# Hard-max attention on one core: row runs per partition, transposes in 32 small units, and a plain end loop

## The chip, the cores and the metric

The kernel runs on one core of one Trainium2 chip. The core has a matrix engine (TensorE, PE in the profile, with its weight loads as PEld), a vector engine (VectorE, DVE), an activation engine (ScalarE, ACT), a general engine that also issues indirect DMAs (GpSimd, POOL) and a sync engine that issues DMAs (SP). Each engine runs its own instructions in order and waits for the others on semaphores. The metric is the device time of one execution in microseconds (us).

## The reference

```python
def setup_inputs():
    B, Sq, Sk, D = 4, 4096, 4096, 128
    return {"q": randn(B, Sq, D), "k": randn(B, Sk, D), "v": randn(B, Sk, D)}   # float32

def reference(q, k, v):
    logits = np.matmul(q, k.transpose(0, 2, 1))
    best = np.argmax(logits, axis=-1)
    b_idx = np.arange(q.shape[0])[:, None]
    return v[b_idx, best, :].astype(np.float32)
```

For each of 4 x 4096 queries the key with the largest dot product is found, and the value row of that key is the output. There is no softmax.

## The kernel before, in words

A tile is 128 queries, one to a partition; there are T = 128 tiles, 32 (NQT) to a batch. Keys are taken in groups of four neighbours. For each tile the kernel finds the best group with reduced precision, then the best key of the group, and then fetches that key's value row. Rows where this could be wrong (close rows) are computed again in fp32.

**Screening on PE, ACT and VectorE.** kT and qT hold the transposed keys and queries of a batch in fp16, in two buffers each, so that the next batch is prepared while this one runs. kT holds four blocks of 1024 columns, a column being a group: block 0 and 1 are sum and difference of the group's first two keys, block 2 and 3 those of the other two. `screen(t)` (lines 216 to 220) issues for one half x of the blocks `dpart` (difference product, whose absolute value A is taken by ACT, L198) and `spart` of the tile before (sum product, L189, plus A through an identity matmul, L208). Half 0 goes through ACT as E (L211), half 1 stays in PSUM; `fold` (L224, VectorE) takes the larger of both into the upper 16 bits of W, whose lower 16 bits hold the group's number and were written once by an iota (L111). `top` (L227, VectorE) takes the eight largest of W. All PSUM tiles come in turn from one pool of four buffers of 1024 fp32 columns (tag "u", line 44), the small ones of the transposes too.

**Refining on VectorE and POOL.** `gather` reads the best group of each query from a table of key differences k16 by an indirect DMA per tile (L244, POOL, "kg"). `dots` multiplies with the queries and sums (L259 to L268), for two tiles at a time. `pick` (L278 to L298) works on a chunk of 8 tiles (4 near the end): it finds the best of the four keys, counts how many are near it (near, CNT), and computes the row of v (win). One indirect DMA per tile (L301, POOL, "vr") fetches the value rows; SP stores a chunk of them (L305). The k16 table is written by `put_k`: a VectorE product kd (L72) and an SP store (L75).

**Close rows.** After half of the tiles `flag_segment`, and after the rest `flags_first` and `flags_last`, collect the rows that are too close (two small matmul groups L349/L350 and L372, in the end phase L450, L465, L491), read their record (FR), query (FQ) and three groups of keys (FK) by indirect DMAs, compute exactly (`exact`, L516 to L535), fetch the value rows (FV) and scatter them over the output. The scatter has to come after all stores of the ordinary rows. `all_rows` is a fallback that the input of this case doesn't enter.

**What sets the order.** The program text does, engine by engine. The loop over `it` (lines 657 to 682) issues for tile `it`: loads on POOL (keys of the next batch at qt 2 to 9, queries at qt 12 to 19), one transposing unit (`unit_k`, 512 columns, at qt 10 to 17; `unit_q`, 512 columns, at qt 18 to 25), the screening, the fold of the tile before, one step of each of the waiting generators (dots, pick, flags; `step`), the top of the tile before that, its gathers, and in `issue` one "kg" and one "vr" gather on POOL. In batch 0 `trn_q` brings 1024 columns of queries at tiles 2, 4 and 6. Before the loop `trn_half` transposes the first keys (lines 148 to 154).

A transposing matmul of keys writes every fourth column of its PSUM tile, since a partition of natk holds 16 neighbouring keys, that is four groups:

```python
o = ps[:, m::4]                                                 # unit_k
nc.gpsimd.iota(out=W.bitcast(U16)[:, 0::2], pattern=[[-1, NG]], base=NG - 1, channel_multiplier=0)
```

Tile t of a batch holds the queries t * 128 to t * 128 + 127, one to a partition, so a query load or an output store has runs of one row (512 bytes in fp32).

After the loop (lines 684 to 726) the end phase is written out by hand: the last tops, all group gathers that are left ahead of the value gathers, then for each chunk its dots, its pick and some value gathers; for the last chunk the counts first, then the close rows' work, whose record and query gathers go ahead of the last three (LATE) value gathers; two of these follow the key gathers, one follows FV, and the scatter is last.

Of the kernel before, what the change touches and what calls it, by code (L numbers as in the profile page):

```python
# [20 lines left out]
QSCALE = 128.0  # L21
TAU = 8.0
NEAR = 0.5
LATE = 3
# [3 lines left out]
def kernel(ctx, tc, q, k, v, out):  # L28
# [36 lines left out]
    def load_q(b, x, y):  # L65
        nc.gpsimd.dma_start(out=natq[b % 2][:, x:y], in_=q[b].rearrange("(t p) d -> p t d", p=P)[:, x:y])  # L66
# [43 lines left out]
    for W in W_t:  # L110
        nc.gpsimd.iota(out=W.bitcast(U16)[:, 0::2], pattern=[[-1, NG]], base=NG - 1, channel_multiplier=0)  # L111
# [31 lines left out]
    def trn_half(b, u, h):  # L143
        x = 2 * (u // 2)
        if h == 0:
            tk_t[u] = pp.tile([P, 1024], FP32, tag="u", name=f"tk_{b}_{u}")
        ps = tk_t[u]
        for m in range(4):
            o = ps[:, h * 512 + m:(h + 1) * 512:4]
            nc.tensor.matmul(out=o, lhsT=natk[b % 2][:, h, 4 * m + x, :], rhs=identh, start=True, stop=False)  # L150
            nc.tensor.matmul(out=o, lhsT=natk[b % 2][:, h, 4 * m + x + 1, :],
                             rhs=identn if u % 2 else identh, start=False, stop=True)
        if h == 1:
            nc.scalar.activation(out=kT[b % 2][:, u * 1024:(u + 1) * 1024], in_=ps, func=AF.Copy)

    def unit_k(b, u, h):
        x = 2 * (u // 2)
        ps = pp.tile([P, 512], FP32, tag="u", name=f"uk_{b}_{u}_{h}")
        for m in range(4):
            o = ps[:, m::4]  # L160
# [3 lines left out]
        nc.scalar.activation(out=kT[b % 2][:, u * 1024 + h * 512:u * 1024 + (h + 1) * 512], in_=ps, func=AF.Copy)  # L164

    def unit_q(b, g):
        ps = pp.tile([P, 512], FP32, tag="u", name=f"uq_{b}_{g}")
        for i in range(4):
            nc.tensor.matmul(out=ps[:, i * P:(i + 1) * P], lhsT=natq[b % 2][:, g * 4 + i, :], rhs=identh,  # L169
                             start=True, stop=True)  # L170
        nc.scalar.activation(out=qT[b % 2][:, g * 512:(g + 1) * 512], in_=ps, func=AF.Copy, scale=QSCALE)  # L171
# [61 lines left out]
    def gather(c, t0, n):  # L233
# [16 lines left out]
        start(dots(c, t0, n), "dots", c)  # L250
# [20 lines left out]
    def pick(c, t0, t1):  # L271
# [8 lines left out]
        near = sp.tile([P, n, 4], FP32, tag=f"near{n}", name=f"near_{c}")  # L280
        nc.vector.scalar_tensor_tensor(out=near, in0=d, scalar=NEAR, in1=mx.to_broadcast([P, n, 4]),
                                       op0=OP.add, op1=OP.is_ge)
        yield "dve",
        nc.vector.tensor_reduce(out=CNT[:, t0:t1], in_=near, axis=AX_X, op=OP.add)
        done.add(("cnt", c))
        yield "cnt",
# [17 lines left out]
        def store():  # L304
            nc.sync.dma_start(out=out[b, qt * P:(qt + n) * P, :].rearrange("(j p) d -> p j d", p=P), in_=vr)  # L305
            done.add(("out", c))

        stores.add(store)
        late_q.append(store)

# [5 lines left out]
    def flag_segment(t0, t1, ready, stored):  # L316
# [62 lines left out]
        nc.vector.scalar_tensor_tensor(out=rw[:, 1:2], in0=tp[:, 0:1], scalar=float(P), in1=tp[:, 1:2], op0=OP.mult, op1=OP.add)  # L379
        yield "dve", 0.17  # L380
        row = fp.tile([P, 1], U32, tag="row", name=f"row_{t0}")
        nc.vector.scalar_tensor_tensor(out=row, in0=rw[:, 1:2], scalar=-float(P), in1=rw[:, 0:1], op0=OP.add, op1=OP.add)
# [44 lines left out]
    LF = {}  # L427

    def flags_first(t0, t1):
        S = t1 - t0  # L430
        H = LF["H"] = fp.tile([P, S, 4], U32, tag="H", name="H_e")
        nc.vector.tensor_scalar(out=H, in0=TOP.bitcast(U32)[:, t0:t1, 0:4], scalar1=16, scalar2=None,
                                op0=OP.logical_shift_right)
        F = LF["F"] = fp.tile([P, S], FP32, tag="F", name="F_e")
        nc.vector.scalar_tensor_tensor(out=F, in0=H[:, :, 1], scalar=TAU, in1=H[:, :, 0], op0=OP.add, op1=OP.is_ge)

    def flags_last(t0, t1, win_last, late):
        S = t1 - t0
        H, F = LF["H"], LF["F"]
        nc.vector.scalar_tensor_tensor(out=F, in0=CNT[:, t0:t1], scalar=1.5, in1=F, op0=OP.is_gt, op1=OP.max)  # L440
        Ec = fp.tile([P, S], FP32, tag="Ec", name="Ec_e")
        nc.vector.tensor_tensor(out=Ec, in0=F, in1=codes[:, t0:t1], op=OP.mult)
        e8 = fp.tile([P, 8], FP32, tag="e8", name="e8_e")
        nc.vector.max(out=e8, in_=Ec)
        val = fp.tile([P, 8], FP32, tag="val", name="val_e")
        nc.vector.tensor_scalar(out=val, in0=e8, scalar1=0.5, scalar2=None, op0=OP.is_gt)
        n2 = fp.tile([P, 3], FP32, tag="n2", name="n2_e")
        nc.vector.tensor_reduce(out=n2[:, 0:1], in_=val, axis=AX_X, op=OP.add)  # L448
        ps = pp.tile([P, 1024], FP32, tag="u", name="fp_e")
        nc.tensor.matmul(out=ps[:, 0:1], lhsT=tri, rhs=n2[:, 0:1], start=True, stop=True)  # L450
        win_last()
        bs = fp.tile([P, 1], FP32, tag="bs", name="bs_e")
        nc.vector.tensor_copy(out=bs, in_=ps[:, 0:1])
        posn = fp.tile([P, 8], FP16, tag="posn", name="posn_e")
        nc.vector.scalar_tensor_tensor(out=posn, in0=iota_r[:, 0:8], scalar=bs, in1=val, op0=OP.add, op1=OP.mult)
        rec2 = fp.tile([P, 8, 2], BF16, tag="rec2", name="rec2_e")
        nc.vector.tensor_copy(out=rec2[:, :, 0], in_=e8)
        nc.vector.tensor_copy(out=rec2[:, :, 1], in_=iota_p.to_broadcast([P, 8]))
        OH = fp.tile([P, 8, P], BF16, tag="OH", name="OH_e")
        for z in range(2):  # L460
            nc.vector.tensor_tensor(out=OH[:, 4 * z:4 * z + 4], in0=iota_h.unsqueeze(1).to_broadcast([P, 4, P]),
                                    in1=posn[:, 4 * z:4 * z + 4].unsqueeze(2).to_broadcast([P, 4, P]), op=OP.is_equal)
        ps2 = pp.tile([P, 1024], FP32, tag="u", name="fq_e")
        for s in range(8):
            nc.tensor.matmul(out=ps2[:, 0:2], lhsT=OH[:, s, :], rhs=rec2[:, s, :], start=s == 0, stop=s == 7)  # L465
        nc.vector.tensor_reduce(out=n2[:, 1:2], in_=F, axis=AX_X, op=OP.add)
        tp = fp.tile([P, 2], FP32, tag="tp", name="tp_e")
        nc.vector.tensor_copy(out=tp, in_=ps2[:, 0:2])
        rw = fp.tile([P, 2], FP32, tag="rw", name="rw_e")
        nc.vector.tensor_scalar(out=rw[:, 0:1], in0=tp[:, 0:1], scalar1=0.5, scalar2=float(1 << 20), op0=OP.is_lt, op1=OP.mult)  # L470
        rr = fp.tile([P, 1], U32, tag="rr", name="rr_e")
        nc.vector.scalar_tensor_tensor(out=rr, in0=tp[:, 1:2], scalar=float(T), in1=tp[:, 0:1], op0=OP.mult, op1=OP.add)
        nc.vector.scalar_tensor_tensor(out=rr, in0=rr, scalar=-1.0, in1=rw[:, 0:1], op0=OP.add, op1=OP.add)
        nc.vector.scalar_tensor_tensor(out=rw[:, 1:2], in0=tp[:, 0:1], scalar=float(P), in1=tp[:, 1:2], op0=OP.mult, op1=OP.add)
        row = fp.tile([P, 1], U32, tag="row", name="row_e")
        nc.vector.scalar_tensor_tensor(out=row, in0=rw[:, 1:2], scalar=-float(P), in1=rw[:, 0:1], op0=OP.add, op1=OP.add)

        def get(dst, src, idx, hi):
            nc.gpsimd.indirect_dma_start(out=dst, out_offset=None, in_=src, in_offset=IOA(ap=idx, axis=0),
                                         bounds_check=hi - 1, oob_is_err=False)  # L480

        late(max(0, len([g for g in late_q if g not in stores]) - LATE))
        get(FR, rec, rr, P * T)
        get(FQ, q_flat, row, P * T)
        bo = fp.tile([P, 1], U32, tag="bo", name="bo_e")
        nc.vector.tensor_scalar(out=bo, in0=row, scalar1=Sq.bit_length() - 1, scalar2=NG.bit_length() - 1,
                                op0=OP.logical_shift_right, op1=OP.logical_shift_left)
        F4 = fp.tile([P, S], FP32, tag="F4", name="F4_e")
        nc.vector.scalar_tensor_tensor(out=F4, in0=H[:, :, 3], scalar=TAU, in1=H[:, :, 0], op0=OP.add, op1=OP.is_ge)
        nc.vector.tensor_reduce(out=n2[:, 2:3], in_=F4, axis=AX_X, op=OP.add)  # L490
        nc.tensor.matmul(out=ps[:, 512:515], lhsT=ones, rhs=n2, start=True, stop=True)  # L491
        gi = fp.tile([P, 3], U32, tag="gi", name="gi_e")
        nc.vector.tensor_scalar(out=gi, in0=FR[:, 0:3], scalar1=NG - 1, scalar2=NG - 1, op0=OP.bitwise_and, op1=OP.bitwise_xor)
        gb = fp.tile([P, 3], U32, tag="gb", name="gb_e")
# [264 lines left out]
```

## Time and profile before

| what | value |
|---|---|
| time, median of 3 runs | 502.19 us (502.18 to 502.57) |
| the profiled execution's own time | 502.19 us |
| its span, first to last instruction | 500.3 us |
| busy PE / DVE / ACT / POOL | 400.6 / 419.5 / 394.3 / 312.9 us |
| first fold, last fold (L224) | 20.98 us, 431.75 us |
| last scatter issued (L509) | 486.87 us |
| fold L224, top L227, one | 1.30, 1.22 us |
| A L198, E L211, one | 1.08, 1.08 us |
| key unit's copy L164, query unit's copy L171 (512 columns), one | 0.61, 0.70 us |
| key transposes L161 and L162, query transposes L169, one | 0.30 to 0.31, 0.22 us |
| kg L244, vr L301, one | 0.99, 0.99 us |
| query load L66, key load L63, one | 0.86, 0.60 us |
| DMA packets, bytes | 51703, 43.47 MB |

A duration in the profile covers an instruction from its start to its end; neighbours on an engine overlap, so the distance between two starts is shorter than a duration. Windows and times are counted from the first instruction. PEclk is the clock granted to TensorE in tenths of full speed; it is full until the matmuls end. After the last scatter some 12 us pass with waiting for it and the closing steps of the program.

### The profile page before, as it was taken

How to read it: one execution, taken by the hardware profiler on the slowest of the kernel's cores; microseconds unless marked ns; L12 is line 12 of the kernel's file. 1: busy time of each engine (PE TensorE's matmuls, PEld its weight loads, DVE VectorE, ACT ScalarE, POOL GpSimd, SP SyncE). 2: the span in 40 equal slices, each digit the busy share in tenths (PEclk: the TensorE clock that was granted, in tenths of full speed). 3: DMA queues.
4: the chain of work that ended last, by engine and by line, in shares of the span. 5: the costliest groups of instructions: out<-in, count | busy, mean ns of one | idle time of the engine just before them, and what ended most of it. 6: DMA issues, size and time to landing. Idle time of an engine off the chain costs nothing. (4 is left out here: it accounts for less than half of the span.)

```text
span 500.3 us, 6434 instructions
## 1 busy us (share of the span) xinstructions
PE 400.6 (80%) x1960; PEld 188.2 (38%) x1960; DVE 419.5 (84%) x808; ACT 394.3 (79%) x441; POOL 312.9 (63%) x345
## 2 busy tenths in 40 slices
PE   8899999999999999999999889999888999201000
PEld 5545554444345544443455444333333333001000
DVE  2179999999999899999998889999999999934130
ACT  1999999999999999999999899999878999100000
POOL 9124445566788886667888566666556666677730
PEclk9999999999999999999999999999999999855555
DMA  9705354232555754234657541142311323243320
GB/s 131 132 16 82 78 96 67 54 98 56 118 95 140 132 84 115 58 92 89 121 118 141 85 105 52 47 110 81 86 50 53 101 55 97 66 118 90 104 58 5
DMA packets 51703, 43.47 MB, mean 87 GB/s; under 512 B 24376, under 2 KB 45883, under 8 KB 51664
## 3 DMA queue, kind: packets, MB, share of 16 engines
q0 software_dynamic: 31520, 30.97, 32.3%
q1 hardware_dynamic: 20144, 12.06, 8.3%
q8 instruction: 15, 0.25, 0.2%
q14 instruction: 24, 0.20, 0.1%
HBM read 39.59 MB, written 12.19 MB: 104 GB/s over the span
## 5 line engine op out<-in xcount | busy, mean ns | idle before, releaser
L198 ACT ACTIVATE A<-pd 128x1024 f16<-128x1024 f32 x256 | 267.7, 1082 | 9.4 <-PE pd L189 9.0
L244 POOL DMA_INDIRECT kg<-k,cand x128 | 126.6, 989 | 122.8 <-DVE p L263 27.9
L224 DVE TENSOR_TENSOR W<-psn,E 128x1024 int16<-128x1024 f32 x128 | 166.2, 1299 | 26.9 <-ACT E L211 16.8
L189 PE MATMUL psn<-kT,qT 128*128 128x512 f16 x512 | 151.8, 378 | 19.2 <-ACT A L198 12.2
L189 PEld LDWEIGHTS <-qT 128*128 128x128 f16 x1024 | 99.7, 99 | 160.2 <-issue 72.8
L189 PE MATMUL pd<-kT,qT 128*128 128x512 f16 x512 | 152.5, 379 | 7.5 <-ACT A L198 7.1
L227 DVE MAX8 TOP<-W 128x8 f32<-128x1024 f32 x128 | 155.8, 1217 | 0.0
L208 PE MATMUL psn<-A,identh 128*128 128x512 f16 x512 | 152.1, 378 | 0.0
L301 POOL DMA_INDIRECT vr<-in_v_dram,win x128 | 126.5, 988 | 39.0 <-issue 37.8
L211 ACT ACTIVATE E<-psn 128x1024 int16<-128x1024 f32 x128 | 137.9, 1077 | 7.3 <-PE psn L208 6.8
L208 PEld LDWEIGHTS <-identh 128*128 128x128 f16 x512 | 49.6, 97 | 60.8
L259 DVE TENSOR_TENSOR prod<-kg,natq 128x768 f16<-128x768 f16 x64 | 34.8, 546 | 0.2 <-issue 0.2
L161 PE MATMUL uk<-identh,natk 128*128 128x128 f16 x96 | 22.2, 303 | 0.2 <-ACT A L198 0.2
L66 POOL DMA_DIRECT2D natq<-in_q_dram x26 | 22.2, 856 | 0.1
L263 DVE TENSOR_TENSOR p<-prod 128x384 f16<-128x384 f16 x64 | 22.2, 349 | 0.0
L268 DVE TENSOR_REDUCE D<-p 128x6 f32<-128x192 f16 x64 | 21.3, 335 | 0.0
L450 PE MATMUL fp_e<-n_e,tri 128*128 128x1 f32 x2 | 0.6, 362 | 23.9 <-DVE n_e L448 23.9
L164 ACT ACTIVATE kT<-uk 128x512 f16<-128x512 f32 x24 | 14.6, 607 | 5.2 <-PE uk L162 4.2
L171 ACT ACTIVATE qT<-uq 128x512 f16<-128x512 f32 x24 | 16.8, 702 | 0.8 <-PE uq L169 0.8
L63 POOL DMA_DIRECT2D natk<-in_k_dram x26 | 15.7, 603 | 0.9 <-POOLq L743 0.8
L266 DVE TENSOR_TENSOR p<-p 128x192 f16<-128x192 f16 x64 | 15.8, 249 | 0.0
L162 PEld LDWEIGHTS <-natk 128*128 128x128 f16 x96 | 12.3, 129 | 3.3 <-issue 1.2
(143 smaller groups left out, 191.8 us busy)
## 6 DMA issues: line engine op xcount, KB each, us to landing
out_dram<-vr SPq DMA_DIRECT2D x13, 512.0 KB, 3.4
k<-kd SPq DMA_DIRECT2D x8, 384.0 KB, 3.0
natk<-in_k_dram POOLq DMA_DIRECT2D x24, 128.0 KB, 3.9
natq<-in_q_dram POOLq DMA_DIRECT2D x24, 128.0 KB, 3.3
kg<-k,cand POOLq DMA_INDIRECT x128, 2.7
vr<-in_v_dram,win POOLq DMA_INDIRECT x128, 2.6
out_dram<-vr SPq DMA_DIRECT2D x6, 256.0 KB, 2.3
natk<-in_k_dram POOLq DMA_DIRECT2D x2, 512.0 KB, 6.2
```

Source lines behind the costliest of these rows:

```text
L66: nc.gpsimd.dma_start(out=natq[b % 2][:, x:y], in_=q[b].rearrange("(t p) d -> p t d", p=P)[:, x:y])
L161: nc.tensor.matmul(out=o, lhsT=natk[b % 2][:, h, 4 * m + x, :], rhs=identh, start=True, stop=False)
L189: nc.tensor.matmul(out=ps[:, n * 512:(n + 1) * 512], lhsT=qT[b % 2][:, qt * P:(qt + 1) * P], rhs=kT[b % 2][:, u * 1024 + n * 512:u * 1024 ...
L198: nc.scalar.activation(out=A, in_=ps, func=AF.Abs)
L208: nc.tensor.matmul(out=ps[:, n * 512:(n + 1) * 512], lhsT=identh, rhs=A[:, n * 512:(n + 1) * 512], start=False, stop=True)
L211: nc.scalar.activation(out=E, in_=ps, func=AF.Relu)
L224: nc.vector.tensor_tensor(out=W_t[t % NW].bitcast(I16)[:, 1::2], in0=ps, in1=E, op=OP.max)
L227: nc.vector.max(out=TOP[:, t, :], in_=W_t[t % NW].bitcast(FP32))
L244: near_q.append(lambda j=j: nc.gpsimd.indirect_dma_start(out=kg[:, j].rearrange("p f d -> p (f d)"), out_offset=None, in_=k16[t0 // NQT], ...
L259: nc.vector.tensor_tensor(out=prod, in0=kg, in1=natq[b % 2][:, x - b * NQT:x - b * NQT + m, :].unsqueeze(2).to_broadcast([P, m, 3, P]), op ...
L263: nc.vector.tensor_tensor(out=p1, in0=prod[:, :, :, 0:64], in1=prod[:, :, :, 64:128], op=OP.add)
L301: late_q.append(lambda j=j: nc.gpsimd.indirect_dma_start(out=vr[:, j, :], out_offset=None, in_=v_flat, in_offset=IOA(ap=win[:, j:j + 1], a ...
```

## The change

1. Layout: partition p of a batch holds the queries 32 p to 32 p + 31, and tile t takes row t of each run. A query load of four tiles then has runs of four rows, and a store of a chunk of n tiles has runs of n rows. The row numbers of close rows are computed differently, with three more small VectorE operations.
2. The columns of kT are in another order: a transposing matmul of keys writes 128 neighbouring columns. The iota that numbers the groups follows this order.
3. The units: `unit_k` and `unit_q` make 256 columns each, 16 and 16 to a batch. Key units come at qt 8 to 30 (two tiles of three), query units at qt 13 to 31 (every third) and at qt 0 to 8 of the batch itself. In batch 0 `unit_q` at tiles 1 to 12 takes the place of three `trn_q`. Query loads come two tiles earlier.
4. `pick` computes win first and the counts of near keys last.
5. The end: `flags_first`, `flags_last` and the hand-written end phase go; both halves use `flag_segment`, and the loop runs on until all is done. Its last chunks have 4, 4, 4, 4, 2, 2, 2, 1, 1 tiles. From tile T + 2 on `issue` takes all group gathers first and two value gathers per round, ahead of those of the close rows; these now come after all value gathers.

The diff, cut to its core:

```diff
     def load_q(b, x, y):
-        nc.gpsimd.dma_start(out=natq[b % 2][:, x:y], in_=q[b].rearrange("(t p) d -> p t d", p=P)[:, x:y])
+        nc.gpsimd.dma_start(out=natq[b % 2][:, x:y], in_=q[b].rearrange("(p t) d -> p t d", p=P)[:, x:y])
...
-        nc.gpsimd.iota(out=W.bitcast(U16)[:, 0::2], pattern=[[-1, NG]], base=NG - 1, channel_multiplier=0)
+        nc.gpsimd.iota(out=W.bitcast(U16)[:, 0::2].rearrange("p (h m r) -> p h m r", h=2, m=4),
+                       pattern=[[-NG // 2, 2], [-1, 4], [-4, P]], base=NG - 1, channel_multiplier=0)
...
         for m in range(4):
-            o = ps[:, h * 512 + m:(h + 1) * 512:4]
+            o = ps[:, h * 512 + m * P:h * 512 + (m + 1) * P]
...
-    def unit_k(b, u, h):
+    def unit_k(b, i):
+        h, u, y = i // 8, i // 2 % 4, i % 2
         x = 2 * (u // 2)
-        ps = pp.tile([P, 512], FP32, tag="u", name=f"uk_{b}_{u}_{h}")
-        for m in range(4):
-            o = ps[:, m::4]
+        ps = pp.tile([P, 256], FP32, tag="u", name=f"uk_{b}_{i}")
+        for m in (2 * y, 2 * y + 1):
+            o = ps[:, (m - 2 * y) * P:(m - 2 * y + 1) * P]
...
-        nc.scalar.activation(out=kT[b % 2][:, u * 1024 + h * 512:u * 1024 + (h + 1) * 512], in_=ps, func=AF.Copy)
+        c = u * 1024 + h * 512 + y * 256
+        nc.scalar.activation(out=kT[b % 2][:, c:c + 256], in_=ps, func=AF.Copy)
...
     def unit_q(b, g):
-        ps = pp.tile([P, 512], FP32, tag="u", name=f"uq_{b}_{g}")
-        for i in range(4):
+        ps = pp.tile([P, 256], FP32, tag="u", name=f"uq_{b}_{g}")
+        for i in range(2):
...
-            nc.sync.dma_start(out=out[b, qt * P:(qt + n) * P, :].rearrange("(j p) d -> p j d", p=P), in_=vr)
+            nc.sync.dma_start(out=out[b].rearrange("(p t) d -> p t d", p=P)[:, qt:qt + n], in_=vr)
...
-    LF = {}
-    def flags_first(t0, t1):
...
-    def flags_last(t0, t1, win_last, late):
...
-    cuts = list(range(0, T - 24 + 1, 8)) + [T - x for x in (20, 16, 12, 8, 4, 0)]
+    cuts = list(range(0, T - 24 + 1, 8)) + [T - x for x in (20, 16, 12, 8, 6, 4, 2, 1, 0)]
...
     def issue(it):
+        if it > T + 1:
+            while near_q:
+                near_q.pop(0)()
+            late = 2
+        else:
+            n = 0
+            while near_q and (n < 1 or near_q[0] in marks):
+                g = near_q.pop(0)
+                n += g not in marks
+                g()
+            late = 2 if n == 0 and len(late_q) + len(fast) > 4 else 1
         for _ in range(late):
-            if fast:
-                fast.pop(0)()
-            else:
-                take_late(1)
-        take_late(0)
+            if fast or late_q:
+                (late_q if late_q and it > T + 1 else fast or late_q).pop(0)()
+            while late_q and late_q[0] in stores:
+                late_q.pop(0)()
...
-    for it in range(T):
-        b, qt = it // NQT, it % NQT
-        elif 12 <= qt < 20:
-            load_part(b + 1, qt - 4)
-            if 10 <= qt < 18:
-                unit_k(b + 1, qt % 4, (qt - 10) // 4)
-            elif 18 <= qt < 26:
-                unit_q(b + 1, qt - 18)
-        if it in (2, 4, 6):
-            trn_q(0, it // 2)
+    it = 0
+    while it < T + 2 or live or fast or near_q or late_q:
+        if it <= T:
+            elif 10 <= qt < 18:
+                load_part(b + 1, qt - 2)
+            if b + 1 < B and qt >= 8 and (qt - 8) % 3 < 2:
+                unit_k(b + 1, (qt - 8) // 3 * 2 + (qt - 8) % 3)
+            if b + 1 < B and qt >= 13 and qt % 3 == 1:
+                unit_q(b + 1, (qt - 13) // 3)
+            if 0 < it < 13:
+                unit_q(0, it + 3)
+            elif 0 < b < B and qt < 9:
+                unit_q(b, qt + 7)
```

## The prediction

> **What bounds the kernel now.** Four views, in this order: the slices by engine, the waits of VectorE, busy time by stage, and the timeline inside one tile. A tile is 128 queries; 128 of them run in 411 of the 500.3 us.
>
> ```profile
> PE   8899999999999999999999889999888999201000
> DVE  2179999999999899999998889999999999934130
> ACT  1999999999999999999999899999878999100000
> PEclk9999999999999999999999999999999999855555
> ...
> DVE W L224 <- ACT E L211: 16.8, 8, 10.7
> DVE W L224 <- PE psn L208: 9.7, 17, 2.1
> ```
>
> Three engines are full for 34 of 40 slices, then comes a tail with little compute. VectorE's fold (L224) waited 26.5 us in all, 10.7 of it before the first fold. So only 15.8 us of waiting lie between the first fold (20.98) and the last (431.75): VectorE is the bound, and no better placing of transposes can return more than that there.
>
> The stages (columns: length, then busy us of PE, PEld, DVE, ACT, POOL, then clock and DMA) tell which tiles wait. Key transposes run in the first, query transposes mostly in the second, none in the last two:
>
> ```profile
> 147.50:181.60 34.10, 33.28 (x184) 17.81 (x183) 32.45 (x60) 32.11 (x39) 27.99 (x29) 1.00 0.62 121
> 181.60:208.00 26.40, 25.46 (x126) 11.11 (x124) 25.32 (x45) 26.40 (x33) 18.23 (x20) 1.00 0.40 88
> 208.00:225.20 17.20, 16.88 (x75) 7.17 (x74) 17.20 (x31) 17.00 (x20) 10.84 (x13) 1.00 0.32 88
> ...
> 385.00:431.70 46.70, 40.28 (x170) 16.34 (x169) 46.70 (x95) 40.04 (x43) 30.10 (x32) 1.00 0.29 77
> ```
>
> With keys PE is fullest and DVE idles 1.65 us, with queries ACT is full and DVE idles 1.1, without either DVE is full. From fold to fold I read 3.45 us a tile with keys, 3.24 with queries, 3.01 without (mean of the first eight tiles of batch 1). The timeline says why:
>
> ```profile
> 167.56 0.31 PE L161 MATMUL uk<-identh,natk 128*128 128x128 f16 x1
> ...
> 167.67 0.31 PE L162 MATMUL uk<-identh,natk 128*128 128x128 f16 x1
> ...
> 187.73 0.39 PE L169 MATMUL uq<-identh,natq 128*128 128x128 f16 x4
> ...
> 188.00 1.31 DVE L224 TENSOR_TENSOR W<-psn,E 128x1024 int16<-128x1024 f32 x1
> 188.35 0.79 ACT L171 ACTIVATE qT<-uq 128x512 f16<-128x512 f32 x1
> ...
> 188.82 1.23 ACT L198 ACTIVATE A<-pd 128x1024 f16<-128x1024 f32 x1
> ...
> 189.76 1.21 ACT L211 ACTIVATE E<-psn 128x1024 int16<-128x1024 f32 x1
> ...
> 191.24 1.31 DVE L224 TENSOR_TENSOR W<-psn,E 128x1024 int16<-128x1024 f32 x1 [0.41 <-PE psn L208]
> ```
>
> Key transposes, whose output steps over four columns, start 0.11 us apart; the query ones, with a dense output, (0.39 - 0.22)/3 = 0.057. Starts on ACT are 0.92 apart for 1024 columns and 0.47 to 0.51 for 512.
>
> In the tail POOL issues one row gather after another, 1.25 us each (0.95 busy, 0.30 issue):
>
> ```profile
> 467.38 1.01 POOL L479 DMA_INDIRECT FR<-rec,rr_e  x1 [0.30 <-issue]
> ...
> 479.75 1.00 POOL L479 DMA_INDIRECT FV<-in_v_dram,xw_fe  x1 [2.48 <-DVE xw_fe L535]
> 481.06 0.94 POOL L301 DMA_INDIRECT vr<-in_v_dram,win  x1 [0.30 <-issue]
> 486.87 1.01 POOL L509 DMA_INDIRECT out_dram<-FV,row_e  x1 [4.87 <-SPq L552]
> ```
>
> FV was read at 479.75, yet the last scatter stood until 486.87, behind the store of the last gathered rows.
>
> **The change, part by part.** The profiled execution took 502.19 us, which is also the median of the runs; its span is 500.3, with 1.9 around it that I leave alone. About 0.2%, 1.0 us, is what a measurement can tell.
>
> *Start.* 64 key transposes now write densely: 64 x 0.05 = 3.4 us off PE. The first 32 (from 7.22) end at 9.0 in place of 10.7, but the second half of the keys has landed only at about 9.1 (VectorE waits for it until 9.10); eight more at 0.057 put the first copy to kT at 9.8, not 11.79. From there ACT is back to back until the first fold, plus one small query copy (0.28) that is now first in line. First fold 20.98 - 2.0 + 0.28 = 19.2: **-1.75**. The query load behind it is safe: its 256-byte writes filled 8.4 to 17.5 us, and as long runs at the rate of the key load (1.05 MB in 5.7 us) it ends near 14 to 16; ACT needs the first unit from it at about 16.9.
>
> *A small unit.* On PE four dense matmuls, 0.23 us, against eight stepped, 0.87. On ACT a 256-column copy. No such row exists; the line through 512 (0.47 to 0.51) and 1024 (0.905 to 0.92) gives 0.25 to 0.30. Bounds: 0.23 (a quarter of 0.92) and 0.51 (no cheaper than a 512 copy). I take 0.28, nearest to the line. ACT then needs 3 x 0.91 + 0.28 = 3.01 a tile, as much as VectorE.
>
> The Trainium skill ("ScalarE: Activation LUTs", Rules for kernel authors) speaks against cutting copies: it budgets about 0.3 us for each ACTIVATE plus 0.83 ns an element, so 0.51 here, and by that ACT would need 3.24 a tile and the total would be near 514. It asks 0.73 for the 512 copy, where the trace has starts 0.47 to 0.51 apart; the measurement decides.
>
> *What a unit tile costs.* About 102 tiles carry a unit (31 in each of batches 0 to 2, 9 in batch 3). A unit takes one of four PSUM buffers, so the second difference product needs the buffer that the fold before last reads, one place earlier than without a unit. Behind the waiting product on PE stand the next sum product and its identity matmuls, and behind them the next fold: 1.31 (fold) + 2 x 0.215 + 4 x 0.215 + 0.2 (pipeline, semaphores) = 2.85 to 2.9 from fold to fold at least. VectorE's light tiles (2.74 to 2.82 in batch 1) can no longer use their speed: with 2.88 as floor the eight tiles give 3.055. The loop ACT's A, PE's next sum, ACT's E, next A comes to 1.1 + 0.92 + 1.02 = 3.04. I take **3.07**; ends 3.01 (no coupling) and 3.24 (the row with one query unit per tile).
>
> *Batch 0.* First seven intervals 22.0 us now (three full query copies); at 3.05 they are 21.35: -0.65. Tiles 8, 9, 11, 12 carry two units, so even the first sum product waits for the fold: up to 1.31 + 2.15 + 0.2 = 3.7; the stretch of six, 20.1 us now, I put at 20.9: +0.8 (bounds -0.6 and +1.5). The other 19, 60.3 now, at 3.07 with 0.95 and more for the kd product (L72) that falls there: -0.8.
>
> *Batch 1.* 101.8 now, of which 2.7 is waiting: 99.1 of VectorE work, plus 32 x 0.045 of lost light tiles, plus 0.6 for its one tile with two units: 101.1, **-0.7**.
>
> *Batch 2.* 107.2 now, 4.9 of it waiting, mostly around the close-row matmuls of the first half (L349, L372). Work 102.3, +1.4, +0.6; of the waits I keep half, for those matmuls and their buffer stay in PE's line: 106.9, **-0.3**. *Batch 3*, nine units where VectorE was full: 9 x 0.05, **+0.45**. Three more tiny VectorE operations per close-row pass and the order of near and win: **+0.3**; win earlier is worth nothing, for POOL has a backlog.
>
> *Layout.* Query loads, moved two tiles earlier on POOL, become runs of 2 KB like the key loads: 0.83 to 0.60 us of POOL for each of 24, 5.5 us. Nothing: POOL is not the bound before the tail, and its order of one group and one value gather per tile keeps the same backlog; without that cover the gain is 5.5. Stores on SP become long runs (landing 3.4 us now); nothing waits for them but the last scatter and, in the tail, a reused buffer, 10 us later.
>
> *Tail.* From the fold of tile 126 (427.73) to FR: now 39.65. After: the group gather of tiles 124 and 125 waits for its index until about +6.0 (two folds, two MAX8 and the small work between); then kg, vr, kg, vr, kg, kg and 23 vr at 1.25 each, FR at 6.0 + 36.25 = +42.25. VectorE's close-row work starts after its last small chunk, near +15, and needs 7 to 8 us: hidden under those 23 gathers; if that cover went, it would cost up to 8. From FR to FV the same 12.4, then FV lands (2.9) and the scatter follows, for all stores are over: 15.5, not 19.5. Sum +2.6 - 4.0 = **-1.2** with rounding; bounds -4.0 and +2.6.
>
> Sum: -1.75 - 0.65 + 0.8 - 0.8 - 0.7 - 0.3 + 0.45 + 0.3 - 1.2 = -3.85: **498.3 us**.
>
> **The rivals.**
>
> *Coupling, slower.* Where ACT, VectorE and the fold loop all need some 3.0 us, the tile settles at the 3.24 of the query stage, or part of the way. Some 95 tiles x 0.17 = +16: 514 in full, 508 halfway. It decides from 3.07 + 3.85/95 = 3.11. For it: ACT already has no idle time at 3.24, and four buffers give little slack. Against: 3.24 is 2.75 + 0.49, ACT's own sum, so the buffers cost next to nothing there.
>
> *Balance cancels, no change.* Tiles at 3.10 to 3.12: 501 to 503. For: in batches 0 and 1 the waiting to be won outside the start is only some 5 us (2.4 and 2.7).
>
> *All waits go, faster.* Light and heavy tiles average out at 3.03 (95 x -0.04 = -3.8) and the stalls of batch 2 vanish (-2.4): 492.
>
> *The end loses.* If the hand-ordered end hid more than I see (the +2.6 stands, the scatter still waits for a store, -4.0 does not come): 502.3, inside the second case.
>
> **How the numbers follow.** Forecast 0.42, all waits go 0.18, no change 0.13, coupling 0.27. The first two are faster: 0.60; same 0.13; slower 0.27. The forecast's own range, from tile pitch 3.04 to 3.10 and the tail's bounds, is 494 to 501. The range for 8 in 10, 490.5 to 508, reaches past the fast case and to coupling halfway.
>
> **What would show it.** Right: matmuls of uk start about 0.057 us apart; first fold near 19.2; ACT's pitch behind a 256-column copy 0.25 to 0.30; folds 3.05 to 3.1 apart all through batches 0 to 2 with under 8 us of waiting after the first; FR to scatter 15 to 16 us. Wrong: unit tiles at 3.2 with PE waiting for VectorE before pd, a copy pitch of 0.4 or more, a PE stall at the first query unit while the load lands, or POOL idle in the tail before FR.

## The result, and the profile after

The changed kernel takes 495.16 us (median of 4 runs, 494.76 to 495.56), the kernel before 502.38 us beside it (502.18 to 502.59): a ratio of 0.9856, 95% interval 0.9839 to 0.9873. The change is faster by 7.2 us, where 3.9 were predicted; the profiled span went from 500.26 to 492.82 us.

The slices by engine of the changed kernel's page (the same four rows as before):

```profile
PE   6798999999999999999989989999988999010000
DVE  3288999999999999999999989999999999781030
ACT  2999999999999999999999989999987999000000
PEclk9999999999999999999999999999999999655555
```

VectorE is now at nine tenths or more from the fifth slice to the end of the screening, but for one slice. Its waits (columns: us in total, times, longest) say what is left for the fold to wait for:

```profile
DVE W L226 <- ACT E L213: 12.4, 5, 9.6
DVE W L226 <- PE uq L171: 5.7, 6, 2.1
DVE W L226 <- PE psn L210: 1.8, 3, 0.6
```

Of 20.2 us (26.9 before) 9.6 lie before the first fold. Summed from the instructions' own times, VectorE is idle for 7.46 us in the first thirteen fold intervals and for 3.15 in all the others up to tile 126; before, it was 6.7 and 9.5. The gain is there, behind tile 13.

Stages of the changed kernel (columns: length, busy us of PE, PEld, DVE, ACT, POOL, then clock and DMA): a stretch of batch 1 with key and query units, its last tiles, and a stretch of batch 3 without units:

```profile
177.00:204.00 27.00, 25.98 (x135) 11.84 (x134) 27.00 (x51) 27.00 (x37) 17.50 (x19) 1.00 0.28 80
204.00:219.70 15.70, 14.98 (x79) 6.89 (x78) 15.56 (x27) 15.70 (x21) 9.46 (x10) 1.00 0.33 89
330.00:419.00 89.00, 80.75 (x350) 33.40 (x348) 89.00 (x176) 81.25 (x90) 55.55 (x57) 1.00 0.28 77
```

With units VectorE and ACT both look full; without them VectorE alone is. (Instructions of ACT overlap, 1.02 us long and 0.904 apart, so a full row doesn't exclude waits of some hundredths of a us.) The distances between neighbouring starts inside two unit tiles, in the timeline of the changed kernel, tell how much room ACT has:

```profile
185.49 1.02 ACT L200 ACTIVATE A<-pd 128x1024 f16<-128x1024 f32 x1
185.66 0.22 PE L162 MATMUL uk<-identh,natk 128*128 128x128 f16 x1
...
185.72 0.22 PE L163 MATMUL uk<-identn,natk 128*128 128x128 f16 x1
...
186.39 0.39 ACT L166 ACTIVATE kT<-uk 128x256 f16<-128x256 f32 x1
...
186.65 1.04 ACT L200 ACTIVATE A<-pd 128x1024 f16<-128x1024 f32 x1
...
187.62 1.02 ACT L213 ACTIVATE E<-psn 128x1024 int16<-128x1024 f32 x1
...
188.53 1.02 ACT L200 ACTIVATE A<-pd 128x1024 f16<-128x1024 f32 x1
```

From A to A of the next tile: 0.90 + 0.26 + 0.97 + 0.91 = 3.04 us, with one small copy of 0.264 in it. The shortest distance behind 1024 columns in this trace is 0.904, so ACT's own sum is 3 x 0.904 + 0.264 = 2.98 and it has 0.06 us a tile to spare. The key transposes start 0.055 to 0.057 us apart, as close together as the query ones.

The start:

```profile
9.54 1.02 ACT L154 ACTIVATE kT<-tk 128x1024 f16<-128x1024 f32 x1 [7.53 <-PE tk L151]
11.29 0.62 PE L180 MATMUL tq<-identh,natq 128*128 128x128 f16 x8 [1.79 <-DMA natq<-in_q_dram]
11.95 1.02 ACT L182 ACTIVATE qT<-tq 128x1024 f16<-128x1024 f32 x1 [1.38 <-PE tq L180]
```

The keys are ready 2.25 us earlier (9.54 for 11.79), but now the first queries are not: PE waits 1.79 us for their load and ACT 1.38 us behind it. The tail:

```profile
462.82 1.01 POOL L411 DMA_INDIRECT FR<-rec,rr  x1 [0.30 <-issue]
...
468.52 1.00 POOL L411 DMA_INDIRECT FK<-in_k_dram,gb  x1 [0.30 <-issue]
474.67 1.00 POOL L411 DMA_INDIRECT FV<-in_v_dram,xw_f  x1 [5.15 <-DVE xw_f L460]
477.69 1.02 POOL L433 DMA_INDIRECT out_dram<-FV,row  x1 [2.02 <-DMA FV<-in_v_dram,xw_f]
```

The scatter now goes as soon as FV has landed. Ahead of FV, POOL idles for 5.15 us with nothing left to do.

### The profile page after: what moved, and what is told of

The parts are those of the page before. It is cut to its first block, busy times and chain, and to the rows that moved or that the text cites. A ratio compares the mean times of both kernels' runs of the same rounds, so it can differ in the third digit from the quotient of the medians.

```text
span 492.8 us, 6520 instructions
## 1 busy us (share of the span) xinstructions
PE 385.1 (78%) x1960; PEld 174.6 (35%) x1960; DVE 419.6 (85%) x839; ACT 394.8 (80%) x498; POOL 305.7 (62%) x345
## 5 line engine op out<-in xcount | busy, mean ns | idle before, releaser
L200 ACT ACTIVATE A<-pd 128x1024 f16<-128x1024 f32 x256 | 263.1, 1032 | 12.0 <-PE pd L191 11.4
L226 DVE TENSOR_TENSOR W<-psn,E 128x1024 int16<-128x1024 f32 x128 | 166.4, 1300 | 20.2 <-ACT E L213 12.4
L213 ACT ACTIVATE E<-psn 128x1024 int16<-128x1024 f32 x128 | 131.0, 1024 | 1.3 <-PE psn L210 1.3
L261 DVE TENSOR_TENSOR prod<-kg,natq 128x768 f16<-128x768 f16 (+1 forms) x65 | 35.2, 543 | 3.0 <-DMA kg<-k,cand 3.0
L173 ACT ACTIVATE qT<-uq 128x256 f16<-128x256 f32 x60 | 23.7, 394 | 1.1 <-PE uq L171 1.1
L265 DVE TENSOR_TENSOR p<-prod 128x384 f16<-128x384 f16 (+1 forms) x65 | 22.5, 349 | 0.0
L270 DVE TENSOR_REDUCE D<-p 128x6 f32<-128x192 f16 (+1 forms) x65 | 21.6, 334 | 0.0
L166 ACT ACTIVATE kT<-uk 128x256 f16<-128x256 f32 x48 | 18.9, 395 | 0.4 <-PE uk L163 0.4
L171 PE MATMUL uq<-identh,natq 128*128 128x128 f16 x120 | 16.5, 219 | 2.9 <-DMA natq<-in_q_dram 2.9
L171 PEld LDWEIGHTS <-natq 128*128 128x128 f16 x120 | 11.3, 98 | 16.1 <-DMA natq<-in_q_dram 4.3
L162 PE MATMUL uk<-identh,natk 128*128 128x128 f16 x96 | 15.8, 219 | 0.0
```

The costliest lines, as they stand in the source:

```text
L173: nc.scalar.activation(out=qT[b % 2][:, g * 256:(g + 1) * 256], in_=ps, func=AF.Copy, scale=QSCALE)
L200: nc.scalar.activation(out=A, in_=ps, func=AF.Abs)
L213: nc.scalar.activation(out=E, in_=ps, func=AF.Relu)
L226: nc.vector.tensor_tensor(out=W_t[t % NW].bitcast(I16)[:, 1::2], in0=ps, in1=E, op=OP.max)
L261: nc.vector.tensor_tensor(out=prod, in0=kg, in1=natq[b % 2][:, x - b * NQT:x - b * NQT + m, :].unsqueeze(2).to_broadcast([P, m, 3, P]), op ...
L265: nc.vector.tensor_tensor(out=p1, in0=prod[:, :, :, 0:64], in1=prod[:, :, :, 64:128], op=OP.add)
```

## The experiments

They ran on three chips on which engines at times got their instructions late (shown below) and the kernel before took 508.9 to 510.9 us; so total times say little, and kernels are compared by the fold intervals of tiles without such a delay. The changed kernel itself gave this comparison:

> The changed kernel itself, on the chip of the next runs, as their reference: 0.985 to 0.987 of the kernel before, unit tiles of batch 1 at 3.04 to 3.10 us from fold to fold, first fold near 19.7, FR 43 us behind the fold of tile 126.

Measured: 508.55 us, ratio 0.9985 (0.9955 to 1.0016), not 0.985 to 0.987. Leaving out the tiles 51 to 55, 81 to 86, 97 to 103 and 116 to 119, the 104 remaining fold intervals differ from those of the first profile by 0.02 us in sum, so these can be compared across chips. The delays cost 4.1 us around tile 52, 0.9 around 84 and 7.5 around 98; on that chip they eat the whole gain; the 7.2 us were measured where no instruction came late.

**What sets the pace of a unit tile: buffers or ACT?**

```diff
+        px = pp.tile([P, 256], FP32, tag="u", name=f"ux_k{b}_{i}")     # a_ring, the same in unit_q
+        nc.tensor.matmul(out=px[:, 0:8], lhsT=identh, rhs=identh[:, 0:8], start=True, stop=True)
```

> Each unit takes one more of the PSUM buffers (a matmul of 8 columns, some 0.03 us of PE, nothing on ACT). The prediction's loop (the difference product waits for the buffer that a fold reads, with the next sum product behind it): now even the first sum product waits for the fold, and a tile with a unit takes 1.31 + 2.15 + 0.2 = 3.3 to 3.7 us, so 95 tiles x 0.25 to 0.6 = 24 to 57 us more than the changed kernel. Rival (the buffers have slack, since the fold is ready before PE gets there): 108 x 0.03 = 0 to 4 us more, light tiles stay at 2.75 to 2.85.

Measured: 519.03 us, ratio 1.0168 (1.0114 to 1.0223), most of it in delays (5.6 us at tile 51, 8.2 at 97 and 98, 4.5 near 117). In the 104 tiles without them it is 3.34 us longer than the changed kernel, 0.65 of that in tiles 7 to 12; the stretch from tile 32 to 51 takes 60.01 us against 59.75. Light tiles of 2.74 to 2.85 are still there. Spread over some 90 units that is 0.04 us each, where the loop of the prediction asked for 0.25 to 0.6 a tile: the loop through the buffers doesn't bind.

```diff
         nc.scalar.activation(out=kT[b % 2][:, c:c + 256], in_=ps, func=AF.Copy)      # a_copy2, the same in unit_q
+        nc.scalar.activation(out=kT[b % 2][:, c:c + 256], in_=ps, func=AF.Copy)
```

> Each unit's copy on ACT is made twice, 0.264 us more of ACT in each of 108 units. If ACT sets the pace of the unit tiles (3 x 0.905 + 0.264 = 2.98, plus what it can't hide): 0.264 x 95 = 25 us more than the changed kernel, unit tiles at 3.30. If VectorE sets it and ACT has the slack between 2.98 and 3.04 to 3.10: 10 to 18 us more, unit tiles at 3.24. If the loop through the buffers sets it: under 5 us.

Measured: 529.97 us, ratio 1.04 (1.0351 to 1.0448); in the 104 tiles 27.0 us longer than the changed kernel, 5.6 of it between tiles 32 and 51. Nearly every tile with a unit takes 3.44 us, heavy or light. ACT in the timeline of that kernel:

```profile
196.22 1.02 ACT L202 ACTIVATE A<-pd 128x1024 f16<-128x1024 f32 x1
...
197.12 1.03 ACT L215 ACTIVATE E<-psn 128x1024 int16<-128x1024 f32 x1
...
198.02 1.04 ACT L202 ACTIVATE A<-pd 128x1024 f16<-128x1024 f32 x1
...
198.93 0.41 ACT L166 ACTIVATE kT<-uk 128x256 f16<-128x256 f32 x1
...
199.38 0.39 ACT L167 ACTIVATE kT<-uk 128x256 f16<-128x256 f32 x1
...
199.66 1.02 ACT L202 ACTIVATE A<-pd 128x1024 f16<-128x1024 f32 x1
```

0.90 + 0.90 + 0.91 + 0.45 + 0.28 = 3.44: ACT is never held up, and the second copy adds 0.46 to its sum, not 0.264, since it starts 0.45 behind the first one, which writes the same columns. VectorE's light tiles have become 3.44 too, and its idle time returns: 6.14 us between tiles 13 and 32, where the changed kernel has 0.27. The tile grew by 0.40 and not by 0.46. If ACT had set the 3.04 of the changed kernel, the tile would be 3.50; so there VectorE sets it, idle for no more than those 0.27 us and with a mean of 3.04 (batch 1 less its two kd products of 0.95: 97.3 / 32), and ACT at 2.98 stands close behind. This is the second case of the expectation, with a dearer copy: only some 0.06 us more per unit would be free.

**Dense matmuls or small units?**

```diff
-            if b + 1 < B and qt >= 8 and (qt - 8) % 3 < 2:
-                unit_k(b + 1, (qt - 8) // 3 * 2 + (qt - 8) % 3)          # 256 columns
-            if 0 < it < 13:
-                unit_q(0, it + 3)
...
+                if 10 <= qt < 18:
+                    unit_k(b + 1, qt % 4, (qt - 10) // 4)                 # 512 columns, dense
+            if it in (2, 4, 6):
+                trn_q(0, it // 2)
```

> The changed kernel with the units of before in their old places (512 columns, 16 neighbouring tiles per batch, three full query copies in batch 0); dense key output, layout and end loop stay. Theory 1 (small units spread out are what took VectorE's waits away): the 16 tiles with a 512 copy need 3.24 us on ACT where VectorE needs 3.03, some of it absorbed, so +1 us per batch: 498 to 499 us, with 6 to 9 us of waiting before folds after the first eight. Theory 2 (dense output on PE is what did it): 495 to 496, waiting near the 4 us of the changed kernel.

Measured: 511.89 us, ratio 1.0034 (1.0 to 1.0067), with delays of its own. Against the kernel before, dense matmuls and layout, with the old units, shorten tiles 7 to 12 by 0.66 us, the rest of batch 0 by 0.85 and 29 undisturbed tiles of batch 1 by 0.38. Against the changed kernel, these units of 512 make the rest of batch 0 longer by 1.63 and the same 29 tiles by 1.67, but tiles 7 to 12 shorter by 1.49. The small units are worth some 1.6 us in each of these two batches, and at the start of batch 0 they lose it again. That is most of the gain in batch 1 and speaks for the first theory; batch 2 had delays here, so its 2.79 us are not taken apart.

**The start and the layout.**

```diff
-            o = ps[:, h * 512 + m * P:h * 512 + (m + 1) * P]
+            o = ps[:, h * 512 + m // 2 * 256 + m % 2:h * 512 + (m // 2 + 1) * 256:2]     # a_step2, iota to match
```

> The changed kernel, but key transposes write every second column and the group numbers follow. Theory 2: PE pays 0.11 us per matmul again, so a key unit takes 0.44 and not 0.23 us and the start 3.4 us more PE time; 497.5 to 499 us. Theory 1: 16 tiles a batch have 0.2 us more PE where PE has 0.25 us of air, so only the start returns (first fold 1 to 1.5 us later): 496 to 497. If stepping by two costs nothing on PE, 495.2.

Measured: 510.9 us, ratio 1.0015 (0.9987 to 1.0044). An output that steps by two columns is as slow as one that steps by four: key transposes start 0.11 us apart. The first copy to kT is at 11.08 (9.54 in the changed kernel), the first fold at 20.54 (19.70), the tiles from 13 to the end of batch 0 take 0.73 us more. Of 1.54 us on the keys 0.84 reach the first fold: the rest hides behind the wait for the queries. The 0.73 us can't be put down to the step: v_end3 below, whose output is dense, takes 0.64 us more than the changed kernel in the same tiles, and tiles 32 to 49, seven of them with a key unit, take the same with the step (0.02 less). So with small units the dense output is worth something at the start and nothing that this run shows behind it, as the first theory said.

```diff
-        nc.gpsimd.dma_start(out=natq[b % 2][:, x:y], in_=q[b].rearrange("(p t) d -> p t d", p=P)[:, x:y])
+        nc.gpsimd.dma_start(out=natq[b % 2][:, x:y], in_=q[b].rearrange("(t p) d -> p t d", p=P)[:, x:y])
```

> The changed kernel with the queries of a tile in 128 neighbouring rows again, so one-row runs in query loads and stores. Both theories: POOL has air before the tail, so 495 to 496 us; the first query units wait longer for their load (it ended at 17.5 us before the change, 15.2 after), at most +1.5. A rival that puts the gain into POOL and DMA time (5.5 us less on POOL) asks for 498 to 500.

Measured: 507.77 us, ratio 0.9926 (0.9893 to 0.996). PE in its timeline:

```profile
19.12 0.39 PE L171 MATMUL uq<-identh,natq 128*128 128x128 f16 x2 [5.15 <-DMA natq<-in_q_dram]
```

The first small query unit stands ahead of the first sum product on PE and waits 5.15 us for the load with short runs, and the first fold moves to 24.72. That is 5.0 us later, where at most 1.5 were expected. So the long runs are what lets the small units stand at tile 1. Behind the start the layout moves no tile that this run can show: batch 3 up to tile 126 takes 95.56 us (95.49 with long runs) and tiles 64 to 78 the same, while tiles 51 to 53 had delays and tiles 13 to 31 take 1.63 us more, in a stretch where the two runs of v_best below, one kernel with long runs, differ by 1.8 us. That speaks against the rival that puts the gain into POOL and DMA time. And the closing steps after the scatter take 13.51 us here, as before (13.39), where every kernel with the new layout has 15.0 to 15.1; in the records it is mostly two instructions on POOL, 9.06 us in place of 7.75 and 2.39 in place of 2.07.

**The tail.**

```diff
+    LATE = 3
+    late(max(0, len([g for g in late_q if g not in stores]) - LATE))
+    get(FR, rec, rr, P * T)
...
-    cuts = list(range(0, T - 24 + 1, 8)) + [T - x for x in (20, 16, 12, 8, 6, 4, 2, 1, 0)]
+    cuts = list(range(0, T - 24 + 1, 8)) + [T - x for x in (20, 16, 12, 8, 4, 0)]
```

> Layout, dense output and small units as in the changed kernel, with the hand-ordered end of before. By the prediction's term for the tail (-1.2): 496.4 us, with the scatter 59.1 us after the fold of tile 126 and not 58.0. If the closing steps, which are 1.7 us longer in the changed kernel, belong to the end loop: 494.7. If the end loop brought more than the prediction said: 497 or more.

The whole hand-written end is back here, with layout, dense matmuls and small units kept. Measured: 511.3 us, ratio 0.9977 (0.994 to 1.0015). From the fold of tile 126 FR is at +43.27 and the scatter at +61.82, but FR waits 4.4 us there for VectorE, which had late instructions; without it FR would stand 1.25 behind the last value gather, at +39.2, and, with the same 18.55 us behind it, the scatter at +57.8, against +57.97 in the changed kernel. FR to scatter takes 18.55 in place of 14.87, of which 4.5 is the wait for the last store. What the new order wins behind FR it loses ahead of it. By the prediction the old end was to stand at +59.1; 57.8 is an estimate from a disturbed trace, but as far as it goes the end loop by itself is worth nothing.

```diff
+                left = sum(g not in stores for g in late_q)                            # v_end3
+                ahead = it > T + 1 and fast and sent[0] < 5 and left <= 3
...
+                (fast if ahead else late_q if late_q and it > T + 1 else fast or late_q).pop(0)()
```

> Only POOL's order in the tail: the record, query and key gathers of the close rows go ahead of the last three value gathers, which then fall into the 5 us in which POOL waits for FV's rows; the scatter is still last. FR comes 3 x 1.25 = 3.75 us earlier. If POOL's backlog sets the end and the stores are done in time: scatter at +54.2 in place of +57.97 from the fold of tile 126, and the whole 3.75 us (0.7%) shorter than the changed kernel, near 0.978 of the kernel before where the clock is undisturbed. Rival: the scatter then waits for the last store, as it did in the kernel before (4.87 us behind the store there), and 0 to 1 us is left; or VectorE is not ready and FR waits for it.

Measured: 505.52 us, ratio 0.9925 (0.9896 to 0.9954). POOL in its tail (fold of tile 126 at 432.64):

```profile
473.33 1.01 POOL L411 DMA_INDIRECT FR<-rec,rr  x1 [1.39 <-remote]
...
485.66 1.00 POOL L411 DMA_INDIRECT FV<-in_v_dram,xw_f  x1 [1.04 <-DMA out_dram<-vr]
489.80 1.01 POOL L433 DMA_INDIRECT out_dram<-FV,row  x1 [3.14 <-DVEq L477]
```

FR comes at +40.68, 2.4 us earlier than the first profile's +43.10 though it stands idle for 1.39 just before; three value gathers fill the idle time ahead of FV, which is at +53.01. But the scatter, at +57.16, is only 0.8 earlier: it goes 4.15 us behind FV, not 3.0. The last store of ordinary rows was issued at 486.17, 0.5 us behind FV, so the rival, a scatter that waits for the last store, isn't excluded. The 3.75 us came in part; how much the late instructions took can't be told from this chip.

**Emptying POOL's backlog earlier, and late instructions.**

```diff
             late = 2 if n == 0 and len(late_q) + len(fast) > 4 else 1
+            if it > T - 32 and it % 3 == 0 and not fast and len(late_q) > 4:            # v_late3
+                late = 2
```

> In the last 32 tiles every third round issues two value gathers in place of one while more than four are waiting, so that up to 9 of the 23 that are left behind the last group gather go into POOL's idle time of some 0.5 us a tile. If the end is set by that backlog (23 x 1.25 us between the last group gather and FR): FR comes 9 x 1.25 = 11 us earlier and the whole is 8 to 11 us shorter than the changed kernel, since VectorE's close-row work is ready some 17 us before FR. If POOL's idle time is not free (a later group gather holds VectorE's dots, or the DMA queue holds the gathers): 0 to 4 us shorter, with VectorE waiting for kg in the last batch.

Measured: 523.14 us, ratio 1.028 (1.0244 to 1.0315), the opposite of what was expected. The backlog did shrink: behind the last group gather 14 value gathers are left in place of 23. But FR is still at +42.51, now waiting 5.4 us for VectorE, and batch 3 has 21 us of delays. VectorE in the tail:

```profile
472.93 0.26 DVE L265 TENSOR_TENSOR p<-prod 128x192 f16<-128x192 f16 x1 [2.81 <-remote]
474.33 0.26 DVE L265 TENSOR_TENSOR p<-prod 128x192 f16<-128x192 f16 x1 [1.14 <-DVE p L265]
475.73 0.21 DVE L268 TENSOR_TENSOR p<-p 128x96 f16<-128x96 f16 x1 [1.14 <-issue]
477.13 0.21 DVE L268 TENSOR_TENSOR p<-p 128x96 f16<-128x96 f16 x1 [1.20 <-DVE p L268]
```

Small operations that follow each other within 0.1 to 0.4 us in the first profile of the changed kernel come 1.4 us apart, waiting for nothing but themselves. The backlog of value gathers was to be the cover for such work, and here it ends first. That its loss alone makes the wait isn't shown: a_ring and a_step2, with the full backlog, have FR waiting 4.5 and 3.1 us too, while the changed kernel on the same chip as this run has no such wait. Whether the extra gathers also bring the delays of batch 3 on, this run doesn't tell; chance in a single execution it is not, since all six timed runs lie within 522.6 and 524.3.

> The kernel before, profiled on the chip of the other runs, to set tile beside tile: where the granted clock is full, each fold interval should be that of its first profile within 0.03 us; where it falls, the tile is longer. If the changed kernel loses more to such stretches than the kernel before, this one shows fewer or shorter ones than the changed kernel's two (11.9 us in all).

Measured in a single execution: 515.56 us, in a kernel whose other runs there have a median of 508.94. Delays of 7.5 us at tiles 53 to 55, 1.5 at 75 to 77 and 1.4 at 84 to 86; its other tiles are those of its first profile, and the tail to the scatter is 2.8 us longer, 3.3 of it in a wait of FK for VectorE (4.5 for 1.2). The kernel before has such delays too; that it has fewer than the changed kernel isn't shown by one execution that is slower than its median.

**Two edits together.**

```diff
-            if 0 < it < 13:
-                unit_q(0, it + 3)
+            if it in (2, 4, 6):
+                trn_q(0, it // 2)                                                      # v_best: this and v_end3
```

> The same tail, and in batch 0 the old three copies of 1024 columns at tiles 2, 4 and 6 in place of twelve small units at tiles 1 to 12. If the small units there cost what the stage table says (tiles 7 to 12 take 20.95 against 19.46 with the old ones, the first seven 22.08 against 22.00): 1.5 to 1.8 us shorter again, 5.3 to 5.6 shorter than the changed kernel. If the gain comes back as longer tiles later in batch 0, or the first fold waits for the second query load: nothing more than the tail's 3.75.

> The same kernel as in the run before, on whichever chip comes, since on the last chips TensorE's granted clock fell in two or three stretches of some 10 us and covered what the edits do. Where the clock stays full until the matmuls end: tail 3.75 and batch 0 1.1 to 1.6 us shorter than the changed kernel's first profile, that is 490 us and 0.975 to 0.978 of the kernel before. If the edits were worth nothing by themselves: 495 us and 0.985. Where the clock falls again: 0.988 to 0.994, and only tiles with a full clock can be compared.

Measured: 505.12 us, ratio 0.991 (0.9876 to 0.9943), on the chip of v_end3, and 500.93 us, ratio 0.9827 (0.9787 to 0.9867), on another. In the second the fold of tile 32 is at 118.82 us (120.54 in the changed kernel), 1.7 us earlier as expected, and FR at +39.57, 3.5 earlier; of that the scatter keeps 0.8, because VectorE loses 2.6 us ahead of FV in waits for nothing but itself. It is faster than the kernel before on both chips, by 0.9 and 1.7%. Against the changed kernel it was not timed on one chip, nor without late instructions, so by how much it beats that one stays open; by its folds it is 1.7 us ahead at tile 32 and keeps that, outside the delays, up to tile 126.

## Why the prediction was right

The direction and the range held; the sum was 3.6 us short. It came that near partly by luck: the three rows that hold the unit tile (other 19 of batch 0, batches 1 and 2) are 6.0 us better than written, and the other rows together 2.4 worse. Each term, with its stage from fold to fold in the two first profiles:

| step of the prediction | predicted | measured |
|---|---|---|
| first fold | -1.75 | -1.28 |
| first seven intervals | -0.65 | +0.08 |
| tiles 7 to 12 | +0.8 | +0.83 |
| other 19 of batch 0 | -0.8 | -2.48 |
| batch 1 | -0.7 | -2.57 |
| batch 2 | -0.3 | -2.79 |
| batch 3 to tile 126, with the small VectorE operations | +0.75 | +0.19 |
| tail, fold of tile 126 to scatter | -1.2 | -1.17 |
| closing steps | 0 | +1.74 |
| sum | -3.85 | -7.45 |

- **The unit tile at 3.07 was the mis-sized term**, and it is in three rows. The price of a small copy was right (0.28 taken, 0.264 measured), and with it ACT's sum (3.01 taken, 2.98 measured). Wrong was the floor of 2.85 to 2.9 from the fold through the PSUM buffers: it rested on counting buffers, not on a row, and its own terms, of which the 0.2 for pipeline and semaphores stands in no row, add up to 2.80, which would have held back hardly any tile. The extra buffer cost 3.3 us in 104 tiles, not 24 to 57, and light tiles kept 2.74 to 2.85. So VectorE averages heavy and light tiles freely at its own work, 3.04 a tile. The prediction's second loop of 3.04, from A through PE and E to the next A, has the same length, and no run takes the two apart; but VectorE's missing idle time is seen, the loop is only added up. In batch 1 it idles 0.76 us where 2.73 were idle before, and without the 1.4 charged for lost light tiles and the 0.6 for the tile with two units the prediction would have read -2.7.
- **The kd products.** In the row of the other 19 tiles the prediction charged 0.95 and more for a kd product. In both first profiles the two of batch 0 run at tiles 8 and 12, ahead of these tiles: a misreading, and more than half of that row's error of 1.7.
- **Batch 2.** Half of 4.9 us of waiting was to stay; 2.12 stayed. Without the 1.4 and 0.6, which didn't come, the term would have been -2.3, and the rest is 0.3 less waiting and 0.2 of rounding.
- **Tiles 7 to 12** came out as written, and the old units there take 1.49 less. In the first seven the five middle intervals were 3.04 to 3.06 as predicted, but the first took 3.36 and the last 3.47, and these two took the 0.65 back. For the first the trace has a wait of 1.3 us of a query unit for its load, the stall at the first query unit that the prediction named as a sign of being wrong. In the last stand the two units of tile 8, with their copies one behind the other on ACT (38.77 and 39.03); the prediction counted that tile to the next row.
- **First fold.** The keys came when predicted (9.54 for 9.8), but the prediction made ACT run back to back from there and looked only at the second query load. It was the first one that was late (11.29). The stepped matmuls agree: 1.54 us later keys, 0.84 later fold.
- **Tail.** FR later by 3.45 (2.6 predicted), FR to scatter shorter by 4.61 (4.0): both sizes a little low, the sum right. That the end loop brings this 1.2 isn't shown: the run with the old end and everything else new comes to +57.8, by an estimate, which leaves nothing for it.
- **Closing steps** were left alone and cost 1.74 us. That the layout does it is shown by the run with the old one (13.51 us); why these instructions on POOL depend on it is not.
- **The rivals.** Coupling fell: it was to decide from 3.11 a tile, and the tile is 3.04. But the doubled copies show how near it was: 0.46 more ACT a unit gives 27 us in 104 tiles. The fold still waits 10.6 us after the first one, where the prediction wrote under 8, but 6.2 of it lie in the first seven intervals. "All waits go" came nearest in batches 0 to 2, where VectorE idles 3.15 us behind tile 13; its 492 lacked the closing steps and took the start for shorter than it is.
- **The copy rule of the Trainium skill** ("ScalarE: Activation LUTs", Rules for kernel authors) would have put ACT at 3.24 and the time near 514. The row of 0.264 us decides against it here. The page states its 0.3 us for a bias given as a pointer operand; the rows of these copies name no operand but the PSUM tile, so the prediction asked the rule for a case that it may not cover.

## What to carry to other kernels

Two engines that are nearly level at their own sums needn't cost anything together: before a buffer loop is charged as a floor, look whether the light tiles keep their length, or add one buffer and see. When a load moves ahead in an engine's line, ask for the landing of every transfer that now stands behind nothing, the first one too. And work that waits under a backlog is only free while the backlog is there: before taking some of it away, look what stands next behind it, here VectorE's chain of small operations.

## What the runs showed of the hardware that was not expected

**Late instructions.** In the first profile of the changed kernel no wait of PE between 20 and 440 us has "issue" as its reason; on a second chip the same program has, by the waits of PE:

```profile
PE psn L191 <- issue: 8.8, 22, 2.9
```

"issue" means that the engine waited for nothing that the profile shows; that its instructions came late is the reading given to it here, not something seen. PE in the timeline of that run:

```profile
337.78 0.59 PE L191 MATMUL pd<-kT,qT 128*128 128x512 f16 x2 [1.16 <-issue]
341.31 0.59 PE L191 MATMUL psn<-kT,qT 128*128 128x512 f16 x2 [2.94 <-issue]
...
344.27 1.06 PE L191 MATMUL pd<-kT,qT 128*128 128x512 f16 x2
```

First PE stands idle, and then its clock halves: the granted clock is 1.00 until 342, 0.53, 0.50 and 0.50 in the next three stretches of 2 us, 0.76 in the fourth and 1.00 from 350, and a pair of matmuls takes 1.06 us in place of 0.59. The halved clock follows the late instructions; it isn't their cause. The Trainium skill ("TensorE: Matmul & The Clock Gate", Part 1: The HAM clock gate) has half the clock after an idle window of some 3.4 us and the full one after a busy window. The gaps here are 1.16 and 2.94 us with one pair of matmuls between them, so this fits only roughly. What makes the instructions late, and why they fall near the tiles 52 and 98 in most variants of the changed kernel on all three chips, no run here shows. One thing stands beside them: the DMA queue that the profile calls "instruction" starts a block of 8 KB at 185.32 and 341.22 us in that run, the second 0.1 us before PE goes on. In the first profile such blocks come at about the same tiles (184.83 and 330.69) with no delay, and on these chips too most blocks pass without one, so this is a trail to follow and not a cause.

**Stepped PSUM outputs.** Transposing matmuls of 128 fp32 columns start 0.11 us apart with a step of two as with a step of four, 0.055 to 0.057 with none.

**A copy behind a copy.** Behind a small ACT copy (256 columns) the next operation starts after 0.264 us; a second copy to the same columns starts 0.45 us behind the first.
